# 25 low parts of FFN weights made ahead of time and kept in DRAM; five FFN units take a fourth 7-product pair

## The chip, the cores and the metric

The kernel runs on one core of one Trainium2 chip. The metric is the device time of one launch in microseconds (us). The core has five engines that run side by side, each working through its own queue in order: PE (TensorE, the matrix multiplier), DVE (VectorE), ACT (ScalarE), POOL (GpSimd) and SP (SyncE, which here only issues DMAs). They wait for each other through semaphores. PE writes its sums to PSUM; everything else lives in SBUF; weights come from DRAM by DMA.

## The reference

One layer of a streaming encoder, in float32, for 256 positions of width 2048. Cut to what matters:

```python
h = rmsnorm(x, g_mix);  proj = h @ w_in            # q,k,v | q,k,v | two gates
y_sb = stick_breaking_attention(q_sb, k_sb, v_sb)   # 8 heads of 128
y_ca = chunked_relpos_attention(q_ca, k_ca, v_ca, rel_bias)
merged = sigmoid(gate_sb) * (y_sb @ w_sb_out) + sigmoid(gate_ca) * (y_ca @ w_ca_out)
x = x + merged @ w_mix_out
h = rmsnorm(x, g_ffn)
g_ff, u_ff = split(h @ w_ffn_in)                    # 2048 -> 2 x 5632
x = x + (silu(g_ff) * u_ff) @ w_ffn_out             # 5632 -> 2048
h = rmsnorm(x, g_ple)
x = x + sigmoid(h @ w_ple_gate) * (p @ w_ple_in)
out = rmsnorm(x, g_final)
```

## The kernel before

**Three products for one.** Float32 accuracy is reached with PE's faster float32r type: each operand is split into a high part `hi` (a rounded copy, made by ACT) and a low part `lo` (operand minus `hi`, made by DVE, helper `minus`, L256), and a product is three matmuls, high by high, high by low and low by high (`three`, L304 to L306). Activations are split once into tables (`T1`, `T2`, `T3`, with high and low halves side by side); weights are split as they stream in.

**Pieces.** All weights pass in one list, `pieces`, of 512 KB each: two blocks of 128 rows by 512 columns (kind "row", and the units), or four by 256 (kind "feat"). `prefetch` (L407) walks the list: `load` asks SP for the DMA into a `raw` place as long as one is free, `split` makes `hi` and `lo` up to three pieces ahead of PE, and `products` issues the matmuls. There are five `raw` places, one more during the attention stages and two more from the FFN on. There are three pairs of `hi` and `lo` buffers, at times four. A `raw` place is free again when ACT and DVE have read it. `schedule_with_timeline_sim=True` lets the compiler choose the order within each engine's queue, from its own estimate of time; the order on the chip is then fixed.

**Units and 7-product pairs.** A unit (`unit`, L173) computes 256 rows by two column blocks of 512, over 16 row blocks of weights, that is, 8 pairs of row blocks. A pair done plainly is two pieces, one for each column block, and 24 matmuls. A pair listed in `PAIRS` is done as a 2x2 block product with 7 instead of 8 block multiplications: one piece with two raws, and 21 matmuls (`pair_products`, L311). It needs sums and differences of weight blocks, made in `split_pair` (L281 to L300): four subtractions of 512 columns, three casts on ACT and three low parts on DVE; and sums of activation blocks, made once for each pair (`pair_sums`, L838, kept in `FP` and `F_more`). An entry -4 of an order tuple is pair 4 done with 7 products; 1 stands for one plain piece of pair 1.

**Stages, in order.** The start (`w_ple_in`, values of the first mixer, first gate columns, in which `scale_table` also scales `T1`); queries and keys of the first mixer in two halves, with a gate unit between; queries and keys of the second mixer, first half; four gate units; its second half; the mixer outputs `w_sb_out` and `w_ca_out` (four groups each, m = 0 and 1); `w_mix_out`; the FFN in three blocks, 11 first-product units (j = 0 to 10, `w_ffn_in`; j = 0 without pairs, the others with pairs 2, 4 and 6) and six second-product units; the last gate. Attention runs as small tasks between pieces.

**What sets the order around the first gate columns.** `ext` holds the relative bias, extended to 384 columns. POOL's queue loads it (L651), fills its ends with two copies (L653) and stores it to DRAM as `ext_d` (L654), from where the second mixer reads shifted rows. `ext` is a tile of the attention pool `ap`, which opens after the pool `start` has closed, and its place (tag "gates") is the one that `gates` takes afterwards. `gate_post` (L835) is ACT's copy of the first gate columns from PSUM into `gates`:

```python
start.close()
...
ext = ap.tile([P, HEADS, 384], F32, tag="gates", name="ext", bufs=1)
...
gates = ap.tile([P, NT, 2, D], F32, tag="gates", name="gates", bufs=1)
```

The place with tag "x" in the pool `bp` holds `x_` at first, then `room` (L885; part of the sums for the gate units' fourth pair, and work space of their pairs), and from L914 `x_` again, loaded a second time by POOL's queue (L916).

## Time and profile before

| | |
|---|---|
| median of 3 runs | 1458.48 us (1458.12 to 1459.41) |
| the profiled execution's own time | 1467.09 us |
| its span, first to last instruction | 1465.3 us |
| mean granted PE clock | 0.996 |
| PE instructions | 6834 |
| DVE and ACT busy, share of the span | 86% and 57% |
| 16 DMA engines, mean rate | 199 GB/s |

A row of groups names the line, the engine, the operation, what is written and read, the form and the count; behind the bar stand the busy time in us, the mean of one in ns, and the idle time of the engine before these instructions. A row of the timeline gives the start and the length in us, then the same names; in brackets is the engine's idle time before it and what ended it. A row of windows gives, for a stretch of time, its length, then each engine's busy time and count, then the granted PE clock (1.00 is full), the DMA engines' busy share and GB/s. Matmul rows overlap: one lasts 390 ns, but the next one starts about 227 ns after it.

### The profile page before, as it was taken

The page shows a single profiled execution, that of the slowest core. Times are in us where ns is not written, and L with a number is a line of the kernel's source. Part 1 is how long each engine was busy: PE and PEld are TensorE (multiplying, and loading weights), DVE is VectorE, ACT ScalarE, POOL GpSimd, SP SyncE. Part 2 cuts the span into 40 slices and gives each one's busy share as a digit, 9 for nine tenths or more (in the row PEclk, how much of TensorE's full clock was granted, in tenths as well). Part 3 has the DMA queues.
Part 4 walks back from the last instruction along what each step waited for, and adds up shares of the span by engine and source line. Part 5 has one row for each costly group of instructions (what it writes and reads, how often), then busy time and mean ns, then how long its engine had stood idle before and what let it go on. Part 6 is the DMA issues. An engine that isn't in the chain of part 4 may idle for free.

```text
span 1465.3 us, 18699 instructions
## 1 busy us (share of the span) xinstructions
PE 1445.4 (99%) x6834; PEld 1208.2 (82%) x6834; DVE 1253.7 (86%) x1592; ACT 831.7 (57%) x994; POOL 34.4 (2%) x44
## 2 busy tenths in 40 slices
PE   9989999999999999999999999999999999999997
PEld 7878888778888888888888888888888888888886
DVE  6869777988987767888989999999989989999775
ACT  6345555654545665565556655556655556666652
POOL 0400000000000000000000000000000000000100
PEclk9999999999999999999999999999999999999999
DMA  9766555566675555766666566666666666655872
GB/s 319 233 203 206 181 173 166 165 193 210 189 270 163 176 172 176 225 205 182 189 188 208 190 219 190 206 208 193 199 194 217 193 186 212 215 187 173 273 227 74
DMA packets 164731, 291.17 MB, mean 199 GB/s; under 512 B 9024, under 2 KB 42096, under 8 KB 164384
## 3 DMA queue, kind: packets, MB, share of 16 engines
q1 hardware_dynamic: 162528, 281.32, 61.4%
q0 software_dynamic: 2112, 8.68, 1.8%
q8 instruction: 53, 0.87, 0.2%
q14 instruction: 38, 0.31, 0.1%
HBM read 284.19 MB, written 5.77 MB: 198 GB/s over the span
## 4 chain that ended last, share of the span: by engine, by line
PE 95%; DMA 2%; DVE 1%; POOL 1%; ACT 0%; issue 0%; SPq 0%; DVEq 0%; ACTq 0%; POOLq 0%
PE mm L306 66%; PE su L306 13%; PE mm L391 8%; PE mm L393 4%; PE tp L481 1%; POOL ext L653 1%; DMA ext<-in_rel_bias 1%; DMA raw<-in_w_ple_in 1%; DVE lo L256 0%; PE mml L306 0%; DMA ext_d<-ext 0%; DMA raw<-in_w_in 0%; PE yp L708 0%; PE xps L535 0%; ACT hi L276 0%
## 5 line engine op out<-in xcount | busy, mean ns | idle before, releaser
L306 PE MATMUL mm<-hi,T 128*128 128x512 f32 x2636 | 850.5, 390 | 1.2 <-DVE v L853 1.2
L256 DVE TENSOR_TENSOR lo<-raw,hi 128x1024 fp32r<-128x1024 f32 (+1 forms) x517 | 623.6, 1218 | 126.7 <-ACT hi L276 118.0
L276 ACT CAST hi<-raw 128x1024 fp32r<-128x1024 f32 (+1 forms) x377 | 395.1, 1052 | 379.3 <-PE mm L306 253.6
L306 PEld LDWEIGHTS mm<-hi,T 128*128 128x128 f32 x2636 | 494.4, 188 | 104.0 <-DVE v L853 2.0
L306 PE MATMUL mm<-lo,T 128*128 128x512 f32 x1318 | 514.0, 390 | 1.1 <-DVE lo L256 1.1
L306 PEld LDWEIGHTS mm<-lo,T 128*128 128x128 f32 x1318 | 247.5, 188 | 51.8 <-DVE lo L256 1.5
L391 PE MATMUL mm<-T,hi 128*128 128x512 f32 x512 | 181.4, 401 | 6.2 <-ACT hi L276 6.2
L393 PE MATMUL mm<-T,lo 128*128 128x256 f32 x512 | 140.3, 282 | 0.0
L391 PEld LDWEIGHTS mm<-T,hi 128*128 128x128 f32 x512 | 95.3, 189 | 26.9 <-ACT hi L276 6.6
L294 ACT CAST hi<-raw 128x1024 fp32r<-128x1024 f32 x70 | 73.9, 1055 | 76.7 <-DVE raw L256 29.4
L256 DVE TENSOR_TENSOR T<-xf,T 128x1536 fp32r<-128x1536 f32 x62 | 108.8, 1755 | 9.2 <-ACT T L297 8.8
L256 DVE TENSOR_TENSOR xf<-raw 128x512 f32<-128x512 f32 x140 | 96.1, 687 | 16.8 <-DMA raw<-in_w_ffn_in 4.7
L393 PEld LDWEIGHTS mm<-T,lo 128*128 128x128 f32 x512 | 97.2, 190 | 2.9 <-DVE lo L256 0.8
L297 ACT CAST T<-xf 128x1536 fp32r<-128x1536 f32 x62 | 91.9, 1482 | 13.5 <-DVE xf L256 12.1
L291 ACT CAST hi<-raw 128x1024 fp32r<-128x1024 f32 x70 | 73.8, 1054 | 31.8 <-PE mm L306 20.0
L306 PE MATMUL mm<-T,T 128*128 128x512 f32 (+1 forms) x282 | 78.3, 371 | 0.0
L306 PE MATMUL su<-hi,T 128*128 128x512 f32 x172 | 66.8, 393 | 0.0
L306 PEld LDWEIGHTS mm<-T,T 128*128 128x128 f32 x282 | 49.8, 188 | 9.2
L256 DVE TENSOR_TENSOR xf<-raw,xf 128x512 f32<-128x512 f32 x70 | 48.0, 686 | 0.7
L256 DVE TENSOR_TENSOR raw<-raw 128x512 f32<-128x512 f32 x70 | 48.0, 686 | 0.5
L853 DVE TENSOR_TENSOR C<-su,C 128x512 f32<-128x512 f32 x72 | 47.7, 684 | 0.4
L306 PE MATMUL su<-T,FP 128*128 128x512 f32 x174 | 47.4, 389 | 0.0
(282 smaller groups left out, 1255.9 us busy)
## 6 DMA issues: line engine op xcount, KB each, us to landing
raw<-in_w_ffn_in SPq DMA_DIRECT2D x176, 512.0 KB, 4.1
raw<-in_w_in SPq DMA_DIRECT2D x160, 512.0 KB, 4.3
raw<-in_w_ffn_out SPq DMA_DIRECT2D x88, 512.0 KB, 4.4
raw<-in_w_mix_out SPq DMA_DIRECT2D x32, 512.0 KB, 4.4
raw<-in_w_ple_gate SPq DMA_DIRECT2D x32, 512.0 KB, 5.0
raw<-in_w_sb_out SPq DMA_DIRECT2D x16, 512.0 KB, 3.9
raw<-in_w_ca_out SPq DMA_DIRECT2D x16, 512.0 KB, 4.3
x<-in_x SPq DMA_DIRECT2D x4, 512.0 KB, 10.6
```

The costliest lines, as they stand in the source:

```text
L256: return nc.vector.tensor_tensor(out, a, b, ALU.subtract)
L276: state["cast"] = nc.scalar.copy(hi[:, c : c + m], raw[:, c : c + m])
L291: nc.scalar.copy(h1, raw1)
L294: nc.scalar.copy(h2, raw2)
L297: nc.scalar.copy(xh, xf)
L306: state["mm"] = nc.tensor.matmul(ps, u, v, start=first, stop=last, skip_group_check=True)
L391: nc.tensor.matmul(ps, hi[:, i, f], lhs[:, kt, :, :].rearrange("p c s -> p (c s)"), start=a, stop=False)
L393: nc.tensor.matmul(ps[:, :S], lo[:, i, f], lhs[:, kt, 0, :], start=False, stop=z)
L481: nc.tensor.transpose(ps[:, k, t * P : (t + 1) * P], src[:, t, (k0 + k) * P : (k0 + k + 1) * P], ident)
L653: nc.gpsimd.tensor_copy(ext[:, :, c0 : c0 + n], ext[:, :, c : c + 1].to_broadcast((P, HEADS, n)))
L853: nc.vector.tensor_tensor(C[i], q, C[j], ALU.add)
```

## The change

`KEPT` names five plain pieces (pair, column block) of a unit, and `KEPT_UNITS` five units. For these 25 pieces the weight is loaded twice. First a piece of kind "low" is put among the pieces of the second half of the first mixer's queries and keys (5), the first half (4) and the second half (5) of the second mixer's, and the mixer outputs (6 and 5): ACT writes the high part and DVE the low part into `room`, and POOL's queue stores the low part to DRAM (`low_d`). Later, in its unit, the piece is loaded with its low part from `low_d` into a second `raw` place, and ACT copies that to `lo` where DVE subtracted. The five units take the order `IN_ORDER`, with pair 5 as a fourth 7-product pair; `F_in` holds its sums of activations. `room` is in use until the mixer outputs end, so the second load of `x_` moves behind them, and `ext` moves from the place of `gates` to the place "x", between the first `x_` and `room`.

```diff
+IN_PAIRS = (2, 4, 5, 6)
+IN_ORDER = (0, 0, 1, -2, 1, -4, 3, -5, 3, -6, 7, 7)
+KEPT = ((0, 1), (1, 0), (1, 1), (3, 0), (3, 1))
+KEPT_UNITS = (2, 4, 6, 8, 10)
...
+    low_d = dp.tile([P, KEPT_N, 1024], F32, tag="low_d", name="low_d")
...
             state["load"] = dma_w.dma_start(dst, src)
+        if pc.get("low") is not None:
+            raw, _ = load_piece(pc["src"][0], pc["ncol"])
+            pc["raw"].append(raw)
+            state["raw"] += 1
+            dma_w.dma_start(raw, low_d[:, pc["low"], :])
...
+        if pc["g"]["kind"] == "low":
+            i = pc["g"]["index"]
+            hi, lo = room[:, :n], room[:, n * (1 + i % 2) :][:, :n]
+            nc.scalar.copy(hi, raw)
+            minus(lo, raw, hi.bitcast(F32))
+            dma_x.dma_start(low_d[:, i, :], lo.bitcast(F32))
+            return
...
-            pc["split"] = minus(lo[:, c : c + m], raw[:, c : c + m], hi.bitcast(F32)[:, c : c + m])
+            if len(raws) == 2:
+                pc["split"] = nc.scalar.copy(lo, raws[1])
+            else:
+                pc["split"] = minus(lo[:, c : c + m], raw[:, c : c + m], hi.bitcast(F32)[:, c : c + m])
...
-    ext = ap.tile([P, HEADS, 384], F32, tag="gates", name="ext", bufs=1)
+    ext = bp.tile([P, HEADS, 384], F32, tag="x", name="ext")
...
+    def spread_lows(i0, n):
+        new = pieces[i0:]
+        del pieces[i0:]
+        for q, pc in enumerate(new):
+            pieces.append(pc)
+            for _ in range((q + 1) * n // len(new) - q * n // len(new)):
+                index = state["low"] = state.get("low", -1) + 1
...
+                pieces.append(dict(g=g, kts=(), ncol=NB, src=[src], needs=[]))
...
     queries_and_keys(0, 1, sb_tasks)
+    spread_lows(at, 5)
...
     queries_and_keys(1, 0, ca_tasks)
+    spread_lows(at, 4)
...
-    x_ = bp.tile([P, NT, D], F32, tag="x", name="x")
-    for c in range(4):
-        dma_x.dma_start(x_[:, :, c * NB : (c + 1) * NB], xr[:, :, c * NB : (c + 1) * NB])
     queries_and_keys(1, 1, ca_tasks)
+    spread_lows(at, 5)
...
             group("row", wo[0], c * NB, range(8 * m, 8 * m + 8), T2, out_post(m, c), needs=lambda kt: ("y", kt))
+        spread_lows(at, 6 - m)
...
+    x_ = bp.tile([P, NT, D], F32, tag="x", name="x")
+    for c in range(4):
+        dma_x.dma_start(x_[:, :, c * NB : (c + 1) * NB], xr[:, :, c * NB : (c + 1) * NB])
...
+    F_in = lp.tile([P, 2, 4, P], F32R, tag="F_in", name="F_in")
...
-                 pairs=PAIRS if j else (), after=None if j else scale_next)
+                 pairs=PAIRS if j else (), after=None if j else scale_next, order=IN_ORDER if kept else None, lows=kept)
```

**POOL's queue at the start, before.** `onesr`, `tri`, `past` and `below` are constants of the attention pool.

```order
14 L130 TENSOR_TENSOR rstd_mix<-ms_mix,mhalf 128x2
15 L632 CAST onesr<-ones 128x128
16 L635 AFFINE_SELECT tri<-ones 128x128
17 L639 AFFINE_SELECT past<-ones 128x128
18 L651 DMA ext<-in_rel_bias 128x8x192
19 L637 CAST below<-tri 128x128
20 L653 COPY ext<-ext 128x8x127
21 L653 COPY ext<-ext 128x8x65
22 L654 DMA ext_d<-ext 128x3072
```

The same place of POOL's queue in the changed kernel:

```order
14 L136 TENSOR_TENSOR rstd_mix<-ms_mix,mhalf 128x2
15 L681 DMA ext<-in_rel_bias 128x8x192
16 L683 COPY ext<-ext 128x8x127
17 L683 COPY ext<-ext 128x8x65
18 L662 CAST onesr<-ones 128x128
19 L665 AFFINE_SELECT tri<-ones 128x128
20 L669 AFFINE_SELECT past<-ones 128x128
21 L684 DMA ext_d<-ext 128x3072
22 L667 CAST below<-tri 128x128
```

The load and the two copies of `ext` now stand ahead of the attention pool's constants, directly behind the reciprocal root of the first norm.

**POOL's queue from the attention stages to the FFN, before.** `bias` is a shifted row of `ext_d`, for the second mixer's tasks; `x` is the second load of `x_`.

```order
23 L767 DMA bias<-ext_d 128x256 x2
24 L769 MEMSET bias 64x2x64
25 L916 DMA x<-in_x 128x2x512 x4
26 L767 DMA bias<-ext_d 128x256 x2
27 L769 MEMSET bias 64x2x64
28 L767 DMA bias<-ext_d 128x256 x2
29 L769 MEMSET bias 64x2x64
30 L767 DMA bias<-ext_d 128x256 x2
31 L769 MEMSET bias 64x2x64
```

The same place in the changed kernel:

```order
23 L797 DMA bias<-ext_d 128x256 x2
24 L799 MEMSET bias 64x2x64
25 L287 DMA low_d<-room 128x1024 x11
26 L797 DMA bias<-ext_d 128x256 x2
27 L799 MEMSET bias 64x2x64
28 L287 DMA low_d<-room 128x1024 x3
29 L797 DMA bias<-ext_d 128x256 x2
30 L799 MEMSET bias 64x2x64
31 L287 DMA low_d<-room 128x1024 x3
32 L797 DMA bias<-ext_d 128x256 x2
33 L799 MEMSET bias 64x2x64
34 L287 DMA low_d<-room 128x1024 x8
```

The 25 stores stand around the loads of `bias`, and the second load of `x_`, which stood behind the first `bias`, now comes behind all of them, in row 35.

**DVE's queue where FFN unit j = 2 begins, before**, from just behind the scaling of unit 1's result. `lo` is the low part of a weight block, `xf`, `raw` and `T_71` belong to 7-product pairs, `fm` and `T_72` to the table of unit 1's result.

```order
694 L256 TENSOR_TENSOR lo<-raw,hi 128x1024
695 L256 TENSOR_TENSOR xf<-raw 128x512
696 L256 TENSOR_TENSOR lo<-raw,hi 128x1024 x2
697 L256 TENSOR_TENSOR raw<-raw 128x512
698 L256 TENSOR_TENSOR lo<-raw,hi 128x1024
699 L256 TENSOR_TENSOR xf<-raw 128x512
700 L465 TENSOR_TENSOR fm<-af 128x128
701 L256 TENSOR_TENSOR fm<-af 128x128
702 L256 TENSOR_TENSOR T_72<-af,T_72 128x2x256
703 L256 TENSOR_TENSOR xf<-raw,xf 128x512
```

The same place in the changed kernel:

```order
735 L268 TENSOR_TENSOR lo<-raw,hi 128x1024
736 L268 TENSOR_TENSOR T_71<-xf,T_71 128x1536
737 L268 TENSOR_TENSOR xf<-raw 128x512
738 L268 TENSOR_TENSOR lo<-raw,hi 128x1024
739 L268 TENSOR_TENSOR raw<-raw 128x512
740 L495 TENSOR_TENSOR fm<-af 128x128
741 L268 TENSOR_TENSOR fm<-af 128x128
742 L268 TENSOR_TENSOR T_72<-af,T_72 128x2x256
743 L268 TENSOR_TENSOR xf<-raw 128x512
744 L268 TENSOR_TENSOR fm<-fm,af 128x128
745 L268 TENSOR_TENSOR lo<-raw,hi 128x1024
746 L268 TENSOR_TENSOR xf<-raw,xf 128x512
```

Ahead of the row `xf<-raw,xf` stood four rows of `lo`; three stand there now, spread wider, and the first pair's differences (`T_71`) already lie ahead of them, because that pair is one piece nearer to the unit's start.

More of the change, by code (lines that the diff above doesn't have):

```diff
@@ L198, in unit @@
                 begun.add(i)
-                pieces.append(dict(pc, src=[src[b]], block=b, first=i == 0, last=2 * i + 2 == len(kts)))
+                pieces.append(dict(pc, src=[src[b]], block=b, first=i == 0, last=2 * i + 2 == len(kts),
+                                   low=None if lows is None else lows.get((i, b))))
     def banks(g, pool, name, n):
@@ L265, in split @@
             held.popleft()
-        if pc["g"]["kind"] == "unit" and len(raws) == 2:
+        if pc.get("pair"):
             return split_pair(pc, *raws)
-        raw, = raws
+        raw = raws[0]
         n = raw.shape[1]
+        if pc["g"]["kind"] == "low":
[5 more added lines that the diff above has]
+            return
         if pc["g"]["keep"] is None:
@@ L404, in size, with places @@
     def size(pc):
-        return 0 if pc["g"]["keep"] is not None else len(pc["src"])
+        return 0 if pc["g"]["keep"] is not None or pc["g"]["kind"] == "low" else len(pc["src"])
+    def places(pc):
+        return len(pc["src"]) + (pc.get("low") is not None)
     def prefetch():
-        while state["loaded"] < len(pieces) and state["raw"] + len(pieces[state["loaded"]]["src"]) <= RAW + state["places"]:
+        while state["loaded"] < len(pieces) and state["raw"] + places(pieces[state["loaded"]]) <= RAW + state["places"]:
             load(pieces[state["loaded"]])
@@ L411, in prefetch @@
         room = 2 if state["at"] < 4 + KD // 2 else 4 if state["fourth"] is not None else 3
-        while state["split"] < state["loaded"] and state["split"] <= state["at"] + 3:
+        ahead = state["at"] + 3
+        ahead += sum(pc["g"]["kind"] == "low" for pc in pieces[state["at"] : ahead + 1])
+        while state["split"] < state["loaded"] and state["split"] <= ahead:
             pc = pieces[state["split"]]
@@ L440, in flush @@
             prefetch()
+            if pc["g"]["kind"] == "low":
+                state["at"] += 1
+                continue
             products(pc)
@@ L861, in four_buffers @@
         state["fourth"] = more.get
+    lows = [(j, i, b) for j in KEPT_UNITS for i, b in KEPT]
+    def spread_lows(i0, n):
[5 more added lines that the diff above has]
+                index = state["low"] = state.get("low", -1) + 1
+                j, i, b = lows[index]
+                n0 = b * D_FF + j * NB
+                g = dict(kind="low", index=index, keep=None)
+                src = w_ffn_in[0][2 * i * P : 2 * (i + 1) * P, n0 : n0 + NB].rearrange("(k p) n -> p k n", p=P)
+                pieces.append(dict(g=g, kts=(), ncol=NB, src=[src], needs=[]))
     def columns(mixer, b):
@@ L899, in block_kernel @@
     state["fourth"] = None
+    at = len(pieces)
     queries_and_keys(0, 1, sb_tasks)
+    spread_lows(at, 5)
     flush(2.6, in_turn=True)
     drain(6)
+    at = len(pieces)
     queries_and_keys(1, 0, ca_tasks)
+    spread_lows(at, 4)
     flush(2.3, in_turn=True)
@@ L1093, in block_kernel @@
             j = k0 // 4 + c
-            unit(w_ffn_in[0], (j * NB, D_FF + j * NB), range(KD), T3, lambda kt: late["F"][0][kt // 4 - 1], rooms(T1),
+            kept = {(i, b): n for n, (u, i, b) in enumerate(lows) if u == j}
+            unit(w_ffn_in[0], (j * NB, D_FF + j * NB), range(KD), T3,
+                 lambda kt: late["F"][0][IN_PAIRS.index(kt // 2)], rooms(T1),
                  C_slots, mid, (in_post if j else first_post)(T2, c, key, OUT_PAIRS[nk]), lambda kt: ("ffn", kt),
-                 pairs=PAIRS if j else (), after=None if j else scale_next)
+                 pairs=PAIRS if j else (), after=None if j else scale_next, order=IN_ORDER if kept else None, lows=kept)
         last = blk == len(FF_BLOCKS) - 1
```

11 lines of the change are left out of this document (7 added, 4 removed).

## The prediction

> **What bounds the kernel now.** I read the page first, then PE's waits, then the timeline around the longest of them, then windows for each stage.
>
> ```profile
> span 1465.3 us, 18699 instructions
> PE 1445.4 (99%) x6834; PEld 1208.2 (82%) x6834; DVE 1253.7 (86%) x1592; ACT 831.7 (57%) x994; POOL 34.4 (2%) x44
> ```
>
> ```profile
> PE mm L391 <- ACT hi L276: 6.2, 1, 6.2
> PE mm L306 <- DVE lo L256: 1.4, 2, 1.1
> ```
>
> PE is busy for 99% of the span, and the waits view holds one PE wait worth the name, of 6.2 us; the next group has 1.4 us in all. So time goes down only if matmuls go or if that one wait goes. Work on other engines costs nothing until PE has to wait for it. PE's price for a 512-column matmul is the pitch, not the length of a row; the chain of waits gives it best in a long unbroken stretch:
>
> ```profile
> 686.79 35.38 PE mm L306 x156
> ```
>
> 35.38/156 = 0.2268 us.
>
> **The one wait: where it comes from.** PE's rows of the timeline (the 512-column matmuls alone), then ACT's, then POOL's:
>
> ```profile
> 72.35 0.40 PE L391 MATMUL mm<-T,hi 128*128 128x512 f32 x1
> ...
> 72.70 0.39 PE L391 MATMUL mm<-T,hi 128*128 128x512 f32 x1
> ...
> 79.46 1.22 PE L391 MATMUL mm<-T,hi 128*128 128x512 f32 x2 [6.25 <-ACT hi L276]
> ...
> 81.31 0.63 PE L391 MATMUL mm<-T,hi 128*128 128x512 f32 x1
> ...
> 81.95 0.63 PE L391 MATMUL mm<-T,hi 128*128 128x512 f32 x1
> ...
> 82.59 0.63 PE L391 MATMUL mm<-T,hi 128*128 128x512 f32 x1
> ...
> 83.23 0.59 PE L391 MATMUL mm<-T,hi 128*128 128x512 f32 x1
> ...
> 83.78 0.39 PE L391 MATMUL mm<-T,hi 128*128 128x512 f32 x1
> ```
>
> ```profile
> 64.98 1.05 ACT L276 CAST hi<-raw 128x1024 fp32r<-128x1024 f32 x1 [1.66 <-PE mm L306]
> 77.39 1.07 ACT L835 COPY gates<-mm 128x512 f32<-128x512 f32 x2 [11.35 <-DMA ext_d<-ext]
> ...
> 85.55 0.61 ACT L469 CAST room<-work 128x512 fp32r<-128x512 f32 x1
> ```
>
> ```profile
> 36.14 0.73 POOL L130 TENSOR_TENSOR rstd_mix<-ms_mix,mhalf 128x2 f32<-128x2 f32 x1 [32.68 <-DVE ms_mix L129]
> ...
> 49.17 0.96 POOL L651 DMA_DIRECT2D ext<-in_rel_bias  x1
> ...
> 58.62 13.01 POOL L653 COPY ext<-ext 128x1016 f32<-128x1016 f32 x2 [7.69 <-DMA ext<-in_rel_bias]
> 71.93 0.58 POOL L654 DMA_DIRECT2D ext_d<-ext  x1 [0.30 <-POOL ext L653]
> ```
>
> ACT's copy into `gates` needs the place that `ext` still holds until its store to DRAM has landed, just ahead of 77.39. ACT works in order, so it stands idle for 11.35 us with the casts of the next weights behind that copy, and PE, which had two pieces in hand, stops. The chain is POOL's: load at 49.17, copies at 58.62, store at 71.93.
>
> **What the change does there.** `gates` no longer shares a place with `ext`, so the copy waits only for PE's sums. PE would have begun its next matmul at 72.70 + 0.35 = 73.05 (0.35 is the pitch of a 512- and a 256-column matmul, 72.70 - 72.35); it began at 79.46: **6.41 us**. Behind the wait PE is slow. From 79.46 to 83.78 it does six such matmul pairs in 4.32 us, where 6 x 0.35 = 2.10 would do: **2.22 us** more. The windows give the reason, a granted clock of 0.50, and 0.59 in the stretch in which it ends:
>
> ```profile
> 80.00:82.00 2.00, 1.97 (x7) 1.19 (x6) 2.00 (x4) 1.45 (x3) 0.20 (x1) 0.50 0.06 13
> 82.00:84.00 2.00, 2.00 (x8) 1.68 (x8) 2.00 (x3) 0.46 (x1) 0.00 (x0) 0.59 0.88 265
> ```
>
> [...]
>
> What is late next there? `room` now waits for `ext_d`, where it waited for `x_`; before, it was first written at 85.55. And `ext` waits for the last reader of the first `x_`, where it waited for the pool `start` to close. The last transposes of `x_` are these:
>
> ```profile
> 38.44 0.60 PE L535 MATMUL xps<-ident,x 128*128 128x128 f32 x4
> ```
>
> So `ext`'s load can go at about 39, ten us earlier than 49.17, and the store lands at about 67, ten before 77 and well ahead of `room`'s first write, even if that moves up by the 8.6 us. The constants behind the copies in POOL's queue come some 13 us later than now; attention needs them only after the first queries and keys. If `ext`'s load did not move up at all, the store would land at 77 and `room`'s cast, due then, would wait about 1 us on ACT, which PE would hardly see.
>
> **The FFN part.** The rows that price it, from the page's groups and windows of single units:
>
> ```profile
> L256 DVE TENSOR_TENSOR lo<-raw,hi 128x1024 fp32r<-128x1024 f32 (+1 forms) x517 | 623.6, 1218 | 126.7 <-ACT hi L276 118.0
> L276 ACT CAST hi<-raw 128x1024 fp32r<-128x1024 f32 (+1 forms) x377 | 395.1, 1052 | 379.3 <-PE mm L306 253.6
> ...
> L256 DVE TENSOR_TENSOR T<-xf,T 128x1536 fp32r<-128x1536 f32 x62 | 108.8, 1755 | 9.2 <-ACT T L297 8.8
> L256 DVE TENSOR_TENSOR xf<-raw 128x512 f32<-128x512 f32 x140 | 96.1, 687 | 16.8 <-DMA raw<-in_w_ffn_in 4.7
> ...
> L297 ACT CAST T<-xf 128x1536 fp32r<-128x1536 f32 x62 | 91.9, 1482 | 13.5 <-DVE xf L256 12.1
> ```
>
> ```profile
> 225.00:285.00 60.00, 58.90 (x324) 50.70 (x323) 49.75 (x68) 36.45 (x46) 0.00 (x0) 1.00 0.57 171
> ...
> 470.00:525.00 55.00, 55.00 (x286) 46.79 (x285) 42.07 (x66) 34.45 (x57) 2.61 (x6) 1.00 0.56 167
> 525.00:575.00 50.00, 50.00 (x238) 41.74 (x237) 34.90 (x42) 31.29 (x44) 0.00 (x0) 1.00 0.57 177
> ...
> 894.20:936.40 42.20, 42.20 (x192) 34.97 (x191) 38.56 (x43) 23.28 (x26) 0.00 (x0) 1.00 0.64 200
> ...
> 979.10:1021.70 42.60, 42.60 (x194) 35.37 (x193) 41.06 (x54) 26.02 (x30) 0.00 (x0) 1.00 0.66 200
> ```
>
> PE: a fourth pair costs 21 matmuls instead of 24, so five units lose 15 x 0.2268 = **3.40 us**. DVE, each of these units: the pair adds four subtractions of 0.687 and one low part of 1.755, 4.50 us; five low parts of 1.218 go, 6.09 us; net 1.59 less. In the window from 979.1, DVE is busy 41.06 of 42.60 us and PE does not wait at all, so a DVE that does less bears a unit shortened by 0.68. ACT gets five copies of 1.05 and one cast of 1.48, 6.7 us: 23 to 26 becomes 30 to 33 of 41.5, hidden. A pair's seven DVE operations come to 4 x 0.687 + 2 x 1.218 + 1.755 = 6.94 us, against a PE time of 21 x 0.2268 = 4.76 for it; between pairs there now always stands a kept piece, which gives PE 2.72 us and DVE nothing, so 6.94 meets 7.48. I take nothing for this.
>
> **The low parts made ahead.** Each is one ACT cast (1.05), one DVE subtraction (1.22), a load and a store of 512 KB. PE sees none of them itself. In the window from 225, DVE goes from 49.75 of 60 to 49.75 + 4 x 1.22 = 54.6, a share of 0.91; in that from 470, from 42.07 of 55 to 49.4, 0.90. Both stay below the 0.96 at which PE still ran unbroken in the FFN, and neither holds a `hi` or `lo` buffer. Without that cover, all 25 would cost 25 x 2.27 = 57 us; I take 0, because of the idle time ahead of ACT's casts in these stages:
>
> ```profile
> 436.79 1.05 ACT L276 CAST hi<-raw 128x1024 fp32r<-128x1024 f32 x1 [3.90 <-PE mm L391]
> ```
>
> Five units' sums for pair 5 are made once, in unit 0, by six DVE operations of at most 0.69 us (the row at 62.38 below), so 4 us at most, beside a unit of 16 plain pieces. The stores queue on POOL around the loads of `bias`, 11, 3, 3 and 8 of them, so a `bias` load waits at most for the subtraction of the store just ahead of it. Two low tiles alternate, so a store has two intervals of some three pieces (3 x 2.72 us) to land in. The second load of `x_` comes behind the last store, near 575 instead of 419:
>
> ```profile
> x<-in_x POOLq DMA_DIRECT2D x4, 512.0 KB, 8.2
> ```
>
> Landed by some 590, it is first read where the first `w_mix_out` unit ends, a unit of about 40 us behind 575.
>
> **Sum.** 6.41 + 2.22 + 3.40 = 12.03 us. The profiled execution took 1467.09 us, so it would be 1455.1 with a span of 1453.3. The median of the runs shown is 1458.48, 0.6% under the profiled one; in the same ratio the changed kernel's median is **1446.5 us**, 0.82% less.
>
> **Rivals.** (a) The wait goes, but the matmuls saved are given back: a pair that comes one piece sooner behind a unit's start, or the four low parts in the stage from 225, in which PE already waits for DVE (58.90 of 60). That leaves 1458.5 - 8.6 = 1450, and 1455 if these four low parts (4.9 us) come on top. Against it stands DVE's smaller load.
>
> (b) The move of `ext` doesn't free ACT, since another wait takes its place (the first weights compete with `ext`'s load, or `room` is late): 3.4 us alone are gained, 1455. Against it: the store has ten us in hand.
>
> (c) Slower: the `raw` places. A kept piece takes two, so 21 loads pass 7 places in 41.5 us: 13.8 us for each, where 42.2 x 7/16 = 18.5 were there.
>
> ```profile
> raw<-in_w_ffn_in SPq DMA_DIRECT2D x176, 512.0 KB, 4.1
> ```
>
> ```profile
> DMA to landing us min/median/max: 6.3/9.3/10.7
> ```
>
> A landing takes 4.1 us, and a place is then held for 2.3 (plain: 1.05 + 1.22) to 6.9 (pair), on average (8 x 6.94 + 13 x 2.3)/21 = 4.1. PE begins to wait when a landing takes over 9.7 us. The second row is that of the `raw` loads from 419 to 432, beside the second load of `x_`: so long landings do occur. At 10.7, a unit takes 3 x (10.7 + 4.1) = 44.4, five units 14.5 us more; the mixer outputs, with 5 places, 22 and 21 loads and 2.3 held, 4.4 x 13.0 = 57.2 instead of 55 and 4.2 x 13.0 = 54.6 instead of 50; in all 21 us, 1468. Against it: that needs two megabytes queued at once, while a kept unit asks for 21/16 of a DMA share of 0.64, 0.84 at most.
>
> (d) POOL's long copy of `ext` holds DVE while it runs, now beside DVE's busiest part of the start: DVE would lose up to 12.4 us, PE has 8.2 us in hand (three pieces of 2.72), and 4.2 are lost: 1451. Against it stand DVE's rows in the midst of the copy that lasts from 58.62 to 71.6:
>
> ```profile
> 61.25 1.22 DVE L256 TENSOR_TENSOR lo<-raw,hi 128x1024 fp32r<-128x1024 f32 x1
> 62.38 0.69 DVE L841 TENSOR_TENSOR work<-T 128x512 f32<-128x512 f32 x1
> ```
>
> They last as long as anywhere. [...]
>
> **How the numbers follow.** The forecast has 0.60, (a) 0.20, (b) 0.05, (c) 0.08, (d) 0.03; 0.04 is left for no change. The range goes down to 1443.5, where the 1.4 us in the second row of PE's waits and the 1.1 us that PE lacks in the window from 225 would go as well, and up to 1454.5, near the end of (a). A measurement here tells 0.2% (2.9 us) from no change: faster 0.87, within it 0.05, slower 0.08.
>
> **What would show it.** PE's waits should hold no wait of 6 us, and the granted clock should stay at 1.00 around 80; ACT's `gates` copy should start at about 68. `ext`'s load should start near 39. In units 2, 4, 6, 8 and 10 PE should run unbroken, at 41.5 us from one to the next; loads there should land in under 7 us. If PE waits for `lo` copies or for `xf` that wait for DMAs, (c) is right. I am wrong if PE's idle time after the change is not about 6 us less in all.

## The result, and the profile after

| | before | after |
|---|---|---|
| median | 1458.30 us (4 runs, 1458.04 to 1459.41) | 1476.48 us (4 runs, 1474.90 to 1476.88) |
| ratio | | 1.0121, 95% interval 1.0104 to 1.0139 |
| the profiled execution's own time | 1467.09 us | 1476.35 us |

The change makes the kernel 1.2% slower; the forecast was 0.8% faster, with a range up to 1454.5. The profiled execution of after stands by its runs; that of before stood 8.6 us above its own. So before was profiled once more (e1 below), in an execution of 1458.19 us with a span of 1456.4, and after is compared with that. Of 109 timed executions of before that ran beside the experiments, 6 took 1466.5 to 1468.6 us and the rest 1457.4 to 1460.5 (two of over 3700 us are left out): by its time, the execution whose profile the prediction rested on is one of the few.

The head of after's page, and its PE waits (us in total, times, longest):

```profile
span 1474.6 us, 18940 instructions
...
PE 1448.8 (98%) x6819; PEld 1203.7 (82%) x6819; DVE 1276.5 (87%) x1623; ACT 881.5 (60%) x1050; POOL 38.3 (3%) x69
```

```profile
PE mm L328 <- DVE lo L268: 6.1, 7, 2.8
PE mm L328 <- ACT hi L295: 3.8, 3, 2.3
...
PE mm L328 <- ACT mm L369: 1.1, 1, 1.1
PE bt L770 <- ACT sh L720: 0.8, 1, 0.8
```

The same two views of before, profiled again:

```profile
span 1456.4 us, 18699 instructions
...
PE 1443.3 (99%) x6834; PEld 1207.1 (83%) x6834; DVE 1254.6 (86%) x1592; ACT 831.2 (57%) x994; POOL 23.4 (2%) x44
```

```profile
PE mm L306 <- DVE lo L256: 1.4, 2, 1.1
PE warm L579 <- POOL mhalf L107: 1.2, 1, 1.2
PE mm L306 <- DVE v L853: 1.0, 2, 0.7
```

There is no wait of 6 us at L391 in this one. After has 15 matmuls less, and yet PE is busy 5.5 us longer and idle 25.8 us (1474.6 - 1448.8) where before, profiled again, has 13.1. About 3 us of the longer busy time are half clock, from 281 to 288 us (a granted clock of 0.50 to 0.59 from 282 on).

To see where the time goes, three rows serve as milestones: the copies that ACT makes when a unit's first sums are done, with first and last start. The view by source line, after and then before profiled again:

```profile
L881 ACT COPY C<-su x18: 569/575/590, 623.8 to 1363.5; 128x512 f32<-128x512 f32 x18
L881 ACT COPY gates<-su x3: 579/589/589, 341.2 to 416.4; 128x512 f32<-128x512 f32 x3
L881 ACT COPY v<-su x2: 574/582/589, 144.6 to 299.9; 128x512 f32<-128x512 f32 x2
```

```profile
L851 ACT COPY C<-su x18: 572/578/589, 606.4 to 1345.1; 128x512 f32<-128x512 f32 x18
L851 ACT COPY gates<-su x3: 581/589/589, 333.7 to 408.9; 128x512 f32<-128x512 f32 x3
L851 ACT COPY v<-su x2: 569/579/589, 144.1 to 292.4; 128x512 f32<-128x512 f32 x2
```

From the first `v` copy to the last `gates` copy is stage I (queries and keys (0,1) and (1,0), where (m, h) is half h of mixer m, and the gate units behind them; nine low parts are made here). From there to the first `C` copy is stage II (queries and keys (1,1), the mixer outputs and the first `w_mix_out` unit's start; sixteen low parts). From there to the first `sgr` activation is stage III, the FFN in the main (no low part is made, 25 are used):

```profile
L1176 ACT ACTIVATE sgr<-mm,rstd_ple x8: 477/690/692, 1401.1 to 1460.6; 128x512 f32<-128x512 f32 x7, 128x256 f32<-128x256 f32 x1
```

| us | up to the first `v` copy | I | II | III | behind it |
|---|---|---|---|---|---|
| before, again | 144.1 | 264.9 | 197.5 | 776.3 | 73.7 |
| after | 144.6 | 271.7 | 207.5 | 777.2 | 73.5 |
| difference | +0.6 | +6.8 | +10.0 | +0.9 | -0.2 |

The lengths are worked out from starts to a hundredth of a us. The two stages in which low parts are made lose 16.8 us, and the FFN, which should have gained 3.4, loses 0.9.

### The profile page after: what moved, and what is told of

The parts are those of the page before. It is cut to its first block, busy times and chain, and to the rows that moved or that the text cites. A ratio compares the mean times of both kernels' runs of the same rounds, so it can differ in the third digit from the quotient of the medians.

```text
span 1474.6 us, 18940 instructions
## 1 busy us (share of the span) xinstructions
PE 1448.8 (98%) x6819; PEld 1203.7 (82%) x6819; DVE 1276.5 (87%) x1623; ACT 881.5 (60%) x1050; POOL 38.3 (3%) x69
## 5 line engine op out<-in xcount | busy, mean ns | idle before, releaser
L328 PE MATMUL mm<-hi,T 128*128 128x512 f32 x2566 | 834.0, 391 | 6.6 <-ACT hi L295 3.8
L268 DVE TENSOR_TENSOR lo<-raw,hi 128x1024 fp32r<-128x1024 f32 (+1 forms) x492 | 592.5, 1217 | 73.9 <-ACT hi L295 61.7
L328 PEld LDWEIGHTS mm<-hi,T 128*128 128x128 f32 x2566 | 480.9, 188 | 110.9 <-ACT hi L295 7.2
L295 ACT CAST hi<-raw 128x1024 fp32r<-128x1024 f32 (+1 forms) x367 | 383.3, 1049 | 257.3 <-PE mm L328 167.9
L328 PE MATMUL mm<-lo,T 128*128 128x512 f32 x1283 | 501.6, 391 | 5.4 <-DVE lo L268 5.3
L268 DVE TENSOR_TENSOR T<-xf,T 128x1536 fp32r<-128x1536 f32 x67 | 117.5, 1754 | 15.2 <-ACT T L319 15.1
L316 ACT CAST hi<-raw 128x1024 fp32r<-128x1024 f32 x75 | 78.9, 1052 | 78.0 <-DVE raw L268 45.8
L413 PEld LDWEIGHTS mm<-T,hi 128*128 128x128 f32 x512 | 94.1, 188 | 19.9
L319 ACT CAST T<-xf 128x1536 fp32r<-128x1536 f32 x67 | 99.1, 1480 | 15.8 <-DVE xf L268 14.0
L313 ACT CAST hi<-raw 128x1024 fp32r<-128x1024 f32 x75 | 78.8, 1051 | 36.0 <-PE mm L328 18.6
L268 DVE TENSOR_TENSOR room<-raw,room 128x1024 fp32r<-128x1024 f32 x25 | 30.6, 1225 | 34.8 <-ACT room L285 34.8
L285 ACT CAST room<-raw 128x1024 fp32r<-128x1024 f32 x25 | 26.2, 1050 | 53.7 <-DMA raw<-in_w_ffn_in 50.5
```

The source lines that it names most:

```text
L268: return nc.vector.tensor_tensor(out, a, b, ALU.subtract)
L285: nc.scalar.copy(hi, raw)
L295: state["cast"] = nc.scalar.copy(hi[:, c : c + m], raw[:, c : c + m])
L313: nc.scalar.copy(h1, raw1)
L316: nc.scalar.copy(h2, raw2)
L319: nc.scalar.copy(xh, xf)
```

## The experiments

Each ratio is to the kernel before, run on the same chip beside it, with its 95% interval. Stage lengths are from each run's own profile, one execution, by the same rows; after and e3, which have the same pieces in stages I and II, differ by more than a us in each (271.7 and 270.5, 207.5 and 209.2), so in a stage that loses much a difference of a us says little. The table has all runs; what each was for follows it. "Order" is the number of `mm` products that stand, in the order of PE's instructions, between the last attention step's `zp` and its first `bt` in stage I, and "ACT at low DMAs" is the wait of ACT's cast of a low part for that part's load or for a store (the waits view from 400 to 640 us).

| run | median us | ratio | I | order | II | ACT at low DMAs in II | III |
|---|---|---|---|---|---|---|---|
| e1, before again | 1458.55 | 1.0009 [0.9997, 1.0020] | 264.9 | 59 | 197.5 | - | 776.3 |
| e2, `ext` alone | 1458.27 | 0.9992 [0.9975, 1.0009] | 265.2 | 59 | 197.4 | - | 776.3 |
| e3, lows made, unused | 1475.81 | 1.0127 [1.0112, 1.0143] | 270.5 | 37 | 209.2 | 34.8 | 776.7 |
| e4, FFN part alone | 1460.36 | 1.0011 [0.9999, 1.0022] | 265.5 | 59 | 197.2 | - | 778.3 |
| e5, work without transfers | 1465.37 | 1.0042 [1.0030, 1.0054] | 270.6 | 33 | 197.8 | 0 | 776.5 |
| e6, loads without work | 1459.97 | 1.0004 [0.9993, 1.0015] | 264.8 | 59 | 197.6 | - | 777.5 |
| e7, one place of its own | 1473.08 | 1.0099 [1.0066, 1.0132] | 272.6 | 21 | 204.4 | 28.6 | 776.3 |
| e8, FFN part, units 4 and 8 | 1459.10 | 1.0000 [0.9987, 1.0013] | 265.2 | 59 | 197.6 | - | 775.0 |
| e9, no wait on landing | 1466.80 | 1.0059 [1.0044, 1.0075] | 271.0 | 33 | 198.2 | 0 | 776.5 |
| e10, two places | 1481.29 | 1.0153 [1.0139, 1.0166] | 276.9 | 43 | 208.5 | 34.5 | 776.2 |
| e11, none in (1,0) | 1468.69 | 1.0070 [1.0056, 1.0084] | 266.7 | 59 | 205.1 | 37.4 | 776.2 |
| e12, 4 and 8, two places | 1462.45 | 1.0035 [1.0022, 1.0047] | 270.2 | 45 | 197.5 | 6.9 | 775.0 |
| e13, loads ahead | 1473.54 | 1.0107 [1.0090, 1.0123] | 272.1 | 33 | 204.1 | 21.2 | 776.2 |
| e14, sixteen, ahead | 1461.74 | 1.0022 [1.0013, 1.0031] | 264.9 | 59 | 199.5 | 19.9 | 776.2 |
| e15, 4 and 8, ahead | 1456.63 | 0.9983 [0.9970, 0.9995] | 264.8 | 59 | 197.4 | 14.7 | 774.9 |
| e16, 4, 5 and 8, ahead | 1457.21 | 0.9994 [0.9986, 1.0003] | 264.8 | 59 | 198.2 | 23.0 | 774.7 |
| e17, work, old order | 1460.43 | 1.0016 [1.0006, 1.0025] | 267.2 | 59 | 198.0 | 0 | 776.3 |
| e18, work, new order | 1465.07 | 1.0044 [1.0027, 1.0061] | 269.4 | 37 | 197.9 | 0 | 776.3 |

**e1 and e2: is the stall there at all?** e1 is before without an edit; e2 has one line of the change.

```diff
-    ext = ap.tile([P, HEADS, 384], F32, tag="gates", name="ext", bufs=1)
+    ext = bp.tile([P, HEADS, 384], F32, tag="x", name="ext")
```

> The kernel before, unchanged, profiled once more. Theory A (the 8.6 us at 73 to 84 us stand in every execution): the profile again shows PE waiting about 6 us at L391 behind ACT, POOL's first copy at L653 about 12 us long, and a span of about 1465 us; the timed runs at 1458 would then be faster for some other reason. Theory B (they stood only in the one execution that was profiled): POOL's copy takes 1 to 2 us, the store of ext lands before 70 us, PE has no wait above 3 us, and the profiled execution is within 2 us of the timed runs, near 1458.

> Of the change only ext's new place. Theory A (the stall stands in every execution): 8.6 us less, a ratio of 0.994. Theory B (it stood in one profiled execution alone): a ratio within 0.998 to 1.002, since ext's store lands in time in either place.

Theory B in both: no stall in e1's profile, and `ext`'s new place alone gives nothing. POOL's two copies took 2.19 us in e1, where they took 13.01 in the first profile. By tile (least, median and greatest ns, first and last start), the first profile and e1:

```profile
L653 POOL COPY ext<-ext x2: 625/6529/12433, 58.6 to 71.0; 128x1016 f32<-128x1016 f32 x1, 128x520 f32<-128x520 f32 x1
```

```profile
L653 POOL COPY ext<-ext x2: 1078/1119/1160, 57.3 to 58.4; 128x1016 f32<-128x1016 f32 x1, 128x520 f32<-128x520 f32 x1
```

DVE's rows beside them differ as well (timeline). First the first profile, where POOL's first copy stands from 58.62 to 71.05: a row just ahead of it, and the end of DVE's unbroken run:

```profile
58.10 0.28 DVE L465 TENSOR_TENSOR work<-work 128x128 f32<-128x128 f32 x1
...
68.67 1.28 DVE L820 TENSOR_TENSOR T<-T,p2bc 128x512 fp32r<-128x512 f32 x2
69.88 0.28 DVE L256 TENSOR_TENSOR work<-work 128x128 f32<-128x128 f32 x1
79.44 1.22 DVE L256 TENSOR_TENSOR lo<-raw,hi 128x1024 fp32r<-128x1024 f32 x1 [9.28 <-ACT hi L276]
```

Then DVE's rows in e1, where it stands from 57.31 on:

```profile
53.83 1.29 DVE L820 TENSOR_TENSOR T<-T,p2bc 128x512 fp32r<-128x512 f32 x2 [0.18 <-PE mm L306]
...
56.88 2.12 DVE L820 TENSOR_TENSOR T<-T,p2bc 128x512 fp32r<-128x512 f32 x2
58.93 0.71 DVE L465 TENSOR_TENSOR work<-work 128x128 f32<-128x128 f32 x1
59.76 1.22 DVE L256 TENSOR_TENSOR lo<-raw,hi 128x1024 fp32r<-128x1024 f32 x1
```

In e1 POOL's first copy begins in the midst of DVE's row of 56.88, and DVE's rows are longer there: 2.12 us, where the same two instructions took 1.29 three us before, and 0.71, where L465 took 0.28 in the first profile. In the first profile the copy fell due while DVE ran two-input instructions without a gap, and it was done 0.9 us after DVE's last one had ended at 70.16. So in these two traces either the copy or DVE's row is stretched while both are under way: the copy, at 12.43 us, where it came late, and DVE's rows, at 2.12 and 0.71, where it came 1.3 us sooner. What stretches the one or the other is not shown; no run here forces the one or the other order.

**e3 and e4: which half of the change costs?** e3 leaves the FFN units as before; e4 makes no low part and loads the weight in its place.

```diff
-                 pairs=PAIRS if j else (), after=None if j else scale_next, order=IN_ORDER if kept else None, lows=kept)
+                 pairs=PAIRS if j else (), after=None if j else scale_next, order=None, lows=None)
```

```diff
-            dma_w.dma_start(raw, low_d[:, pc["low"], :])
+            src = w_ffn_in[0][2 * i * P : 2 * (i + 1) * P, n0 : n0 + NB]
+            dma_w.dma_start(raw.rearrange("p (k n) -> p k n", n=NB), src.rearrange("(k p) n -> p k n", p=P))
...
-    spread_lows(at, 5)
```

> The change without its FFN part: ext moved, the second load of x_ moved, the 25 low parts made and stored, but the FFN units as before (their low parts subtracted, three pairs each). If making the low parts is what costs, and ext gives nothing: 1458 + 17 = 1475 us, ratio 1.012, with the loss in the stages of queries, keys and mixer outputs. If the FFN part is what costs: 1458 or less. My prediction's reading, that PE sees none of the making: 1450 (A) or 1458 (B).

> The change without the making: the five FFN units take four pairs and copy a second loaded piece in place of their five subtractions; what is loaded is the weight itself and not its low part, so a part of the product is computed from other numbers. All loads, copies and matmuls of those units are as in the changed kernel. If the FFN part does what I predicted: 3.4 us less than ext alone, ratio about 0.9977 under theory B. If the saving is given back there (waits for the second loads, xf, the first pair): 1458 or more, ratio 1.000 to 1.002. If the places of raw bound it (rival c): 1465 to 1473.

The making costs 17.4 us against e1's and e2's 1458.4. The FFN part alone costs about 2, hardly clear of the noise (interval 0.9999 to 1.0022), and its stage III is 2.0 us longer as well. The prediction had nothing for the first and a gain of 3.4 for the second.

**e5 and e6: work or transfers?** In e5 ACT's cast and DVE's subtraction read columns of `room`; no load, no store. In e6 only the loads are left.

```diff
+                pc["raw"].append(room[:, 3072:].bitcast(F32))
+                continue
...
-            dma_x.dma_start(low_d[:, i, :], lo.bitcast(F32))
```

```diff
-            nc.scalar.copy(hi, raw)
-            minus(lo, raw, hi.bitcast(F32))
-            dma_x.dma_start(low_d[:, i, :], lo.bitcast(F32))
```

> The making of the 25 low parts without its transfers, FFN units as before: ACT's cast and DVE's subtraction stay at their places in the order, but read 1024 columns that lie in SBUF already, so no load, no place of raw, no store (the low parts are of the wrong numbers and unused). Theory W (the 25 x 2.27 us of ACT and DVE work cost): as dear as with the transfers, 1473 to 1477, ratio 1.011 to 1.013. Theory P (the loads through the five places of raw, and their landing, cost): 1457 to 1461, ratio 0.999 to 1.002.

> Only the 25 loads of 512 KB through the places of raw, FFN units as before: nothing reads them, no cast, no subtraction, no store. Theory W: 1457 to 1461. Theory P: most of the 17.5 us, though a place is free when its load has landed, without the wait for ACT and DVE: 1465 to 1475. If neither this nor the work alone costs, it is the two together: ACT and DVE, which work in order, standing at a load that has not landed: both runs near 1460.

Neither theory alone. The work costs 5.7 us in stage I, with the changed order that it brings (e17 and e18 below), and 0.3 in stage II; the loads through the places of `raw` cost nothing in either (264.8 and 197.6; e6's ratio is within its interval of 1, and its 1.2 us more stand in stage III). So the 11.7 us of e3 in stage II need both together, work and transfers. In after's trace one wait of that kind looks like this, by SP's queue, ACT and PE:

```profile
542.31 0.37 SPq L247 DMA_DIRECT2D raw<-in_w_ffn_in  x1
```

```profile
543.71 1.05 ACT L295 CAST hi<-raw 128x1024 fp32r<-128x1024 f32 x1
549.27 1.04 ACT L285 CAST room<-raw 128x1024 fp32r<-128x1024 f32 x1 [4.51 <-DMA raw<-in_w_ffn_in]
550.23 1.04 ACT L295 CAST hi<-raw 128x1024 fp32r<-128x1024 f32 x1
```

```profile
548.63 0.39 PE L328 MATMUL mm<-hi,T 128*128 128x512 f32 x1
551.32 0.73 PE L328 MATMUL mm<-hi,T 128*128 128x512 f32 x2 [2.30 <-ACT hi L295]
```

ACT works in order. It stands 4.51 us at the low part's cast, whose load was issued at 542.31 and is there just ahead of 549.27; the cast that PE needs comes behind it, at 550.23, and PE waits 2.30 us. In all of after's stage II PE is idle for 6.4 us and busy for 3.6 us more than in e1, with 996 matmuls in both and the granted clock at 1.00. No low part is loaded back before 747 us.

**e7, e10 and e13: can the load be ahead?** All make the 25 low parts whole, unused, with POOL's queue loading into `room`: e7 into one place, issued behind the last low part's store; e10 into two places, the low part written over the weight; e13 into two places, high and low part in a third.

The lines of e7, of e10 where they differ from e7's, and of e13:

```diff
+        dma_x.dma_start(room[:, 2048:3072].rearrange("p (k n) -> p k n", n=NB), src.bitcast(F32R))
...
             dma_x.dma_start(low_d[:, i, :], lo.bitcast(F32))
+            if pc["next"]:
+                load_low(i + 1)
```

```diff
+        raw = room[:, 1024 * (1 + index % 2) :][:, :1024]
...
+            minus(raw, raw.bitcast(F32), hi.bitcast(F32))
+            dma_x.dma_start(low_d[:, i, :], raw.bitcast(F32))
+            if pc["next"]:
+                load_low(i + 2)
```

```diff
+            nc.scalar.copy(hl, raw.bitcast(F32))
+            minus(hl, raw.bitcast(F32), hl.bitcast(F32))
+            dma_x.dma_start(low_d[:, i, :], hl.bitcast(F32))
+            if pc["next"]:
+                load_low(i + 2)
```

> The making whole (load, cast, subtraction, store, unused afterwards), but each load goes into a place of its own inside room, is issued by POOL's queue right behind the store of the low part before, and passes neither SP's queue nor the five places of raw. DMA traffic and the work of ACT and DVE are those of the changed kernel. Theory P: 1457 to 1462, ratio 0.999 to 1.003. Theory W, or a theory that the traffic itself slows the other loads: 1473 to 1477.

> The making whole (unused afterwards), each load in one of two places of its own in room, issued by POOL two low parts ahead, so that it has landed some 10 us before ACT's cast; the low part takes its raw place. Theory L: 1464 to 1468, ratio 1.004 to 1.007 (the work's 6.9 us stay). Theory T: 1473 to 1477.

> The making whole (25, unused afterwards), with two places in room for the loads and one for high and low part: POOL issues the load of the low part after next at the moment a subtraction ends, with no store to wait for, so it has two intervals (14 to 20 us) to land. If ACT's standing at these loads is the second share: it stands there for less than 10 us in all, and the time is e9's, 1464 to 1468, ratio 1.004 to 1.007. If the traffic is: 1473 to 1477.

By their times alone e7 would speak for the work or the traffic and e13 for the traffic, and e10 lies above every case. But all three missed what they were built for, since ACT stood at a low part's transfer in another way, so they don't decide. In e7 and e10 it still stood at the load (28.6 and 34.5 us in stage II), which POOL could only issue behind the last subtraction or the last store's landing. In e13 the loads were there, and ACT stood at the store that still read the one place for high and low part. The ACT waits of after and of e13 from 400 to 640 us:

```profile
ACT room L285 <- DMA raw<-in_w_ffn_in: 39.5, 15, 4.9
```

```profile
ACT room L283 <- DMA low_d<-room: 19.4, 13, 4.5
ACT room L283 <- DMA room<-in_w_ffn_in: 1.8, 1, 1.8
```

**e9: all transfers and all work, but no wait of the one for the other.** As e3, with cast and subtraction reading columns of `room`:

```diff
+            raw = room[:, 3072:].bitcast(F32)
             nc.scalar.copy(hi, raw)
             minus(lo, raw, hi.bitcast(F32))
```

> All transfers and all work of the making (25 loads through the places of raw, 25 casts and subtractions, 25 stores, unused afterwards), but cast and subtraction read columns that lie in SBUF already, so ACT and DVE never stand at a low part's own load (the low parts are of the wrong numbers). The work alone cost 6.9 us, the loads alone 1.4. Theory L (the rest is ACT and DVE, which work in order, standing at these loads): 1465 to 1468, ratio 1.005 to 1.007. Theory T (the traffic, with the stores, slows the loads of the weights that PE needs): 1473 to 1477, ratio 1.010 to 1.013.

Theory L. Stage II goes from 209.2 to 198.2, with the same transfers and the same work. So of the 11.7 us that e3 loses there, 11.0 go with ACT's standing at these loads; traffic and work are left with 0.7. What a given standing costs PE is not fixed, though. e13 and e14 make the same sixteen low parts there, ACT stands 21.2 and 19.9 us, and the stage loses 6.6 and 2.0; in e16 ACT stands 23.0 and it loses 0.7. PE's longest wait in the stage is 2.6 us in e13, with half clock behind it (0.50 to 0.67 from 510 to 518), 0.5 in e14 and 0.4 in e16. How much of ACT's standing reaches PE would then depend on what PE has in hand at that moment; no run tries that by itself.

**e11, e17 and e18: what costs in stage I?** e11 is e3 without the four low parts in (1,0). e17 and e18 are e5 without the five in (0,1), and without the four in (1,0).

```diff
     queries_and_keys(1, 0, ca_tasks)
-    spread_lows(at, 4)
```

```diff
     queries_and_keys(0, 1, sb_tasks)
-    spread_lows(at, 5)
+    spread_lows(at, 0)
```

```diff
     queries_and_keys(1, 0, ca_tasks)
-    spread_lows(at, 4)
+    spread_lows(at, 0)
```

> The making as in the changed kernel, FFN units as before, but without the four low parts among the queries and keys of (1,0): 21 are made, the last four of the list are left out. If those four push the last attention step of that stage into the gate unit behind it (PE lost 5.3 us more than before at 270 to 287): 1475.8 - 5.3 = 1470.5, ratio 1.008. If the five of the stage ahead do it: 1475 again.

> As e5 (work of the making alone, on columns that lie in SBUF; no transfers; unused), but none of it in the stage (0,1): four in (1,0) and the sixteen behind. PE's order has 59 products between the last zp and bt, as before the change. Theory O (the order of PE's instructions costs it): the stage from 144 to 409 us keeps its 265 us, the time is 1458 to 1460, ratio 1.000 to 1.001. Theory N (the four parts among the queries and keys (1,0) cost it): 270, and 1463 to 1465, ratio 1.004.

> As e5, but none of the work in the stage (1,0): five in (0,1) and the sixteen behind. PE's order has 37 products between the last zp and bt, as in the changed kernel. Theory O: that stage takes 269 to 272 us, the time is 1463 to 1466, ratio 1.003 to 1.005. Theory N: 265 to 266.7, and 1458 to 1461, ratio 1.000 to 1.002.

e11 is below its lower case: without the four it takes 3.8 us less than e3 in stage I and 4.1 less in stage II, where it has the same sixteen low parts, so a stage's loss also swings by some us with what comes before. Both e17 and e18 come nearer to O than to N, e17 above O's range. Low parts shift where the build puts attention's products among the matmuls. Every run with 59 in the "order" column has a stage I of 264.8 to 267.2 us, every run with 45 or fewer 269.4 to 276.9. It isn't all: e11 and e17 keep the old order and still lose 1.8 and 2.3. With five low parts in that stage, the order goes with 269.4 - 266.7 = 2.7 us (e18 against e11). The orders of ACT and DVE differ between these two as well, and e11 has the transfers, so this is the worth of one whole schedule against another. The four further low parts and all waits at loads together come to 1.1 us (e3 against e18, both with 37), no more than two such profiles can differ by.

What the order does is seen in after's rows. PE, then DVE, then windows (length, PE, PEld, DVE, ACT, POOL busy, clock, DMA share, GB/s):

```profile
274.23 0.50 PE L770 MATMUL bt<-sh,below 128*128 128x512 f32 x1 [0.80 <-ACT sh L720]
...
278.21 0.50 PE L328 MATMUL mm<-hi,T 128*128 128x512 f32 x1 [0.44 <-ACT hi L295]
281.53 0.79 PE L328 MATMUL mm<-lo,T 128*128 128x512 f32 x1 [2.81 <-DVE lo L268]
```

```profile
278.18 0.69 DVE L268 TENSOR_TENSOR xf<-raw 128x512 f32<-128x512 f32 x1 [2.86 <-DMA raw<-in_w_in]
278.79 0.95 DVE L776 TENSOR_TENSOR ls<-ls,bt 128x768 f32<-128x768 f32 x1
279.65 0.69 DVE L268 TENSOR_TENSOR raw<-raw 128x512 f32<-128x512 f32 x1
280.26 1.22 DVE L268 TENSOR_TENSOR lo<-raw,hi 128x1024 fp32r<-128x1024 f32 x1
```

```profile
282.00:284.00 2.00, 2.00 (x6) 1.47 (x6) 2.00 (x5) 0.62 (x1) 0.00 (x0) 0.50 0.66 174
284.00:286.00 2.00, 2.00 (x7) 1.61 (x6) 0.29 (x1) 0.44 (x1) 0.00 (x0) 0.50 0.23 88
286.00:288.00 2.00, 2.00 (x7) 1.57 (x7) 1.31 (x2) 1.67 (x3) 0.00 (x0) 0.59 0.00 0
```

The step's `bt` has so few products ahead of it that PE waits for ACT's `sh`, and its rest falls among the first pairs of the gate unit. There DVE first stands 2.86 us for a load of weights, then has attention's `ls` ahead of the subtraction that PE needs, and PE stands 2.81 us. Half clock from 282 to 288 follows. So the late load has a part in this stop beside the order: in e18, with the same 37 products and no transfers of low parts, DVE does not stand there, and PE's wait at that place is the first row of its waits from 140 to 412 us:

```profile
PE mm L331 <- DVE lo L271: 1.3, 1, 1.3
```

Why that load came late was not followed.

**e8 and e12: which units keep their saving?** e8 is e4 with units 4 and 8 alone; e12 is a whole kernel with these units, its ten low parts made in e10's two places, none in (1,0).

```diff
-KEPT_UNITS = (2, 4, 6, 8, 10)
+KEPT_UNITS = (4, 8)
```

> The FFN part alone as in e4, but for units 4 and 8 only, which do not stand ahead of a block's output units (2, 6 and 10 do); loads in place of low parts are the weight itself, so a part of the product is computed from other numbers. If a unit's saving is given back in the output units behind it (e4's PE lost 3.0 us at 791 to 857, 1.0 at 1067 and 0.6 at 1319 more than before): 6 matmuls x 0.2268 = 1.4 us less than ext alone, 1456.9, ratio 0.999. If every kept unit gives its saving back: 1458.3 to 1459.2, ratio 1.000 to 1.001.

> A whole kernel that may beat both: units 4 and 8 alone take four pairs (in e8's profile their two units lost 1.3 us and gave none back), so ten low parts are made, five among queries and keys (0,1) and five in (1,1), loaded into two places in room two ahead. If the making of ten costs nothing outside the stage (1,0): 1458.3 - 1.3 = 1457.0, ratio 0.999; if the five in (1,1) cost as in the changed kernel (4 us at 492 to 518): 1461, ratio 1.002.

By its median e8 falls into its second case, no gain, and in its profiled execution the start was 2.2 us longer (146.3 us to the first `v` copy); but stage III is 775.0 in both, 1.3 us less than before, where 6 matmuls come to 1.36: units 4 and 8 keep what they save. Units 2, 6 and 10 have a block's output units behind them. In e4 and after PE waits there, and before has no PE wait that the view shows from 640 to 1380 us. After's PE waits in that stretch, and the rows of DVE and ACT around the longest:

```profile
PE mm L328 <- ACT mm L369: 1.1, 1, 1.1
PE mm L328 <- DVE C L883: 0.6, 1, 0.6
PE su L328 <- DVE x L1119: 0.6, 1, 0.6
```

```profile
839.36 1.22 DVE L268 TENSOR_TENSOR lo<-raw,hi 128x1024 fp32r<-128x1024 f32 x1
840.49 0.69 DVE L883 TENSOR_TENSOR C<-su,C 128x512 f32<-128x512 f32 x1
841.09 1.22 DVE L268 TENSOR_TENSOR lo<-raw,hi 128x1024 fp32r<-128x1024 f32 x1
842.22 1.28 DVE L883 TENSOR_TENSOR C<-su,C 128x512 f32<-128x512 f32 x2
```

```profile
839.97 1.48 ACT L319 CAST T<-xf 128x1536 fp32r<-128x1536 f32 x1
841.35 0.58 ACT L369 COPY mm<-x 128x512 f32<-128x512 f32 x1
```

The output unit's first matmul into a bank waits for ACT's copy of `x` into it, which stands behind a pair's cast, while DVE goes from one row to the next without a gap. My reading is that a unit that ends 0.68 us sooner brings these pairs on before DVE and ACT are through, so that the time saved is stood out there, and some more; no run tries one of these units by itself. These waits come to 2.3 us; the other 2.0 of the 4.3 that after gives back (3.4 + 0.9) are busy time of PE that did not go down with the matmuls. e12 is above both of its cases: it lost 5.3 us in stage I, where it has the order of 45 and two places as in e10, which were not separated.

**e14, e15 and e16: a version without these costs?** e13's places, but low parts in stage II alone; e14 makes sixteen unused, e15 uses ten (units 4 and 8), e16 fifteen (units 4, 5 and 8, five low parts in each of the three places). All three leave out the first two `spread_lows`; e15 further:

```diff
-KEPT_UNITS = (2, 4, 6, 8, 10)
+KEPT_UNITS = (4, 8)
...
     queries_and_keys(1, 1, ca_tasks)
-    spread_lows(at, 5)
+    spread_lows(at, 2)
...
-        spread_lows(at, 6 - m)
+        spread_lows(at, (4, 4)[m])
```

> As e13, but only the 16 low parts among the queries and keys (1,1) and the mixer outputs; none in the stages (0,1) and (1,0) ahead of the gate unit (the other nine are left out). If the two shares are all: 1458.3 + 1 (e5's loss at 538 to 546) = 1459 to 1460, ratio 1.000 to 1.002, and PE loses 2.3 us at 274 to 281 as before. If there is a third: 1463 or more.

> A whole kernel: units 4 and 8 take four pairs, ten low parts made as in e14 (two in (1,1), four in each mixer output). By e8's profile 1.3 us gained in the FFN, by e14's expectation up to 1 lost: 1457 to 1458.5, ratio 0.999 to 1.000.

> A whole kernel: units 4, 5 and 8 take four pairs (none stands ahead of a block's output units), fifteen low parts made as in e14, five in each of the three stages. If the units keep their savings: 9 x 0.2268 = 2.0 us gained, up to 1 lost, 1456.3 to 1457.5, ratio 0.9985 to 0.9995. If units 4 and 5 in a row give the saving back: 1458 to 1459.

Stage I is as before in all three. e14 is above its range: stage II is 2.0 us longer, and ACT still stands 19.9 us, 19.0 of them at stores. e15, with ten, loses nothing there, keeps 1.3 us in the FFN, and is the one kernel faster than before: 1456.63, a little below its range, ratio 0.9983, interval 0.9970 to 0.9995. e16's third unit, right behind a kept one, brings 0.2 us more in stage III and its five further low parts cost 0.8 in stage II.

## Why the prediction was wrong, step by step

- **"6.41 us" and "2.22 us", the wait and its half clock.** The rows were read rightly, but they are of an execution such as, by their times, 6 in 109 are. The numbers said so: 1467.09 - 1458.48 = 8.61, and the two terms come to 8.63. The step that failed is "in the same ratio": the difference between profile and median was spread over the whole kernel, where it was this very wait. What is true of the timed runs is 0 (e1, e2). Two of the prediction's signs came true all the same, `ext`'s load at 40.2 and the `gates` copy at 67.5, but they say nothing of the time: in e1, with `ext` in its old place, the copy starts at 67.0.
- **Rival (d), POOL's copy and DVE.** It asked whether POOL holds DVE and found DVE's rows of normal length. It was the other way round in that trace: the copy took 12.43 us beside DVE's run, its store was late, and ACT and PE stood (11.35 and 6.25 us). In after, with the copy moved up, both copies took 1.60 us.
- **"PE sees none of them itself ... I take 0", the low parts made ahead.** This is the step that made the kernel slower: 16.8 us in the profile, 17.4 in e3. The argument went by shares: DVE at 0.91 and 0.90, ACT with idle time ahead of its casts. Shares say whether the work fits, and it does (e9: 0.7 us in stage II). They don't say what stands behind it: ACT, in order, waited 39.5 us in stage II at loads that nobody needs soon, and the casts that PE needs stood behind them. Without these waits the stage loses 0.7 instead of 11.7 (e9 against e3). The prediction named a load for each low part and gave it no price, although its own reading of the `gates` copy, ACT idle in order "with the casts of the next weights behind that copy", was the same mechanism.
- **The order of PE's instructions.** The prediction took the order of attention's products as given. The low parts moved them (59 to 37 products), which goes with 2.7 us where it could be set against the rest (e18, e11); with four or five low parts, some 2 us are lost in stage I with the old order too (e11, e17).
- **Rival (c), the `raw` places, 1468.** It had the stages (it put 21 us down, part of them to the mixer outputs) but not the mechanism. Its condition, landings of over 9.7 us, didn't come in the FFN: from 624 to 1400 us the loads of `raw` land in 3.4 to 8.3 us in after, 4.6 at the median. From 416 to 624 they take up to 10.0, 5.3 at the median, but the loads alone cost nothing in stages I and II (e6).
- **3.40 us, the matmuls saved.** They went (6819 matmuls), and units 4 and 8, inside a block, keep some 0.65 us each (e8, e15). "I take nothing for this" failed at the ends of the blocks: DVE's sum was made over a unit, and the output units behind have no room, as far as their rows tell. Stage III was 2.0 us longer in e4 and 0.9 in after, so 5.4 and 4.3 us were given back, more than rival (a) had.
- **Taken for harmless, and rightly:** `ext`'s new place (0.9992, within its interval of 1) and, with no PE wait that the rows show, pair 5's sums and the second load of `x_`.

What stays open: how the rest of stage I's loss divides between the order, the work and their number (no run that works on nine low parts there has the old order), why the load ahead of 278.18 came late, and which of the FFN's two in-order queues, DVE's or ACT's, comes first at the blocks' ends. None was tried by itself.

## What to carry to other kernels

Set a profiled execution against the timed runs before pricing a term in it: a gap between them that has the size of a wait may be that wait. Work that is moved ahead into idle time is not free if it waits for a transfer: on ACT, in order, everything behind it waited too, and 11.0 of the 11.7 us that e3 lost in stage II went with it; so load it well ahead or don't put it there. And compare the order of instructions on the engine that bounds the kernel, even where the change adds none to it.
